# Samples' new keys in blocks of 32, both prompt blocks at once through the spatial product, values normalised further ahead

## The chip, the cores and the metric

The kernel runs on one core of a Trainium2 chip. The metric is the device time of one execution in microseconds (us), the median of several runs. A profile of one execution gives the time of each instruction on TensorE (PE, with its weight loads as PEld), VectorE (DVE), ScalarE (ACT), GpSimd (POOL) and the DMA queues.

## The reference, cut to what matters

One inference step of a two-layer encoder, for one prompt of 256 positions and 8 samples of 16 new positions each, with 128 cached positions behind every sample. All data are float32. Layer 0 has 8 forgetting-attention heads and 8 stick-breaking heads; layer 1 is a gMLP with a causal spatial product over chunks of 128 positions.

```python
# layer 0, samples: keys are the 128 cached ones and the sample's own 16 new ones
k_all = concatenate([cache_fox_k, gk], axis=1)
v_all = concatenate([cache_fox_v, gv], axis=1)
go = fox_core(gq, k_all, v_all, F_all[:, P:], F_all, qpos, kpos)   # softmax(q k^T + forget bias, causal) v
to = sb_core(tq, sk_all, sv_all, qpos, kpos)                       # stick-breaking weights, strictly causal
hs = hs + (concatenate([go * silu(gz), to * silu(tz)], -1) @ w_out0)

# layer 1
u, v, z = split(rmsnorm(h, norm1_g) @ w_in1)      # 4096 columns each
v = layernorm(v, ln_g, ln_b)                      # over the 4096 columns
mixed = einsum('gts,bnsgc->bntgc', tril(w_sp), v) + b_sp   # 16 groups of 256 columns
h = h + (u * mixed * silu(z)) @ w_out1
```

A sample sees only its own 16 new keys, so of the 128 x 128 scores between all samples' new queries and new keys only eight blocks of 16 x 16 on the diagonal count; the rest is masked.

## The kernel before, in words

**Tokens.** The 384 tokens stand as NT = 3 blocks of 128: two of the prompt, one with all samples (8 x 16). `P` is 128, `T` is 384.

**Dense products.** `dense_nat` multiplies all 384 tokens with 512 columns of a weight. To keep float32 accuracy every operand is split into a high part (fp32r) and the rest, and three products are summed (high x high, high x low, low x high). `wunit` loads a 128 x 512 piece of the weight (`raw`), ScalarE copies it to `whi` (L84), VectorE subtracts to `wlo` (L86), and `products` issues the matmuls at L100, L101 and L102: two pieces a step, three token blocks, 18 matmuls of 512 columns. `whi` and `wlo` have four buffers each.

**Order.** The instructions are traced in program order and then scheduled: each engine gets a fixed order from a simulation, in which an instruction that stands earlier in the program goes first among those that are ready. `tc.issue_after(x)` queues what its block traces on x's engine behind x. Work of the attention is hooked between the steps of later dense products (`between`, `at(g, what, kp, f)`).

**Layer 0.** `quad(g)` does four heads: it projects k, q, z and v and hooks `scores` and `attended` for pairs of heads, (0, 1) and (2, 3). `head` is a generator that is run in pieces:
- `scores`: the cached keys are turned (L625), the prompt scores go to the bank `sc` (L630, L631). In the bank `sd` the samples' new keys give one 128 x 128 product (L633), and the cached keys give four products in tiles of 32 output rows, one for each pair of samples (L636). `scores` runs L630 to L633 inside `issue_after(last_product[0])`. A bias with the mask (`md`, for the samples, 384 wide) is added, the softmax or the stick-breaking runs over 384 columns, and the weights (six blocks of 128, three for the prompt and three for the samples) go to memory (`wd`) and come back in 32-row pieces (`blk`, L496).
- `attended`: `blk` is turned to `PT` (L674). Samples' outputs go to the part `od` of a bank: first the new values by four products of 32 output rows over all 128 new keys (L681), then the cached values, eight more (L685). Then come the prompt's (L687 to L689), and the gate is multiplied in.

**Layer 1.** The eight groups of 512 columns of v are projected first and kept in `vt`, with their statistics. `normalise(c)` loads gain and bias of a group to a slot (L786, L787), does six steps on VectorE (L790, L791) and stores the samples' part. Then, for each group c:
1. the spatial weights of two of the 16 groups are loaded, masked, turned and split (`spatial_weights`),
2. z is projected and put through silu to `gate` (L862), u is projected and multiplied in (L865),
3. `normalise(c + 1)`,
4. the spatial product of the split values `vh`, `vl` for the three token blocks (L885, L886, L887; 256 columns each), whose result is multiplied into `gate` (L890),
5. `gate` is turned by VectorE and 16 small transfers on POOL (`turn`, L125 and L128), split into two slots (`ghi`, `glo`), and `split_values(c + 1)` fills `vh` and `vl`, which have one buffer each,
6. after groups 2, 4 and 6, `out1` multiplies two finished groups with the output weight (evicted at L830).

**Slots.** One pool of 16 slots (`slot()`, 6 KB a partition each) holds, in layer 1, the normalised input in 8 slots, the residual `h1` in 4, `ghi` and `glo` in one each per group until `out1` has read them, and the gain and bias of a group in one.

Of the kernel before, what the change touches and what calls it, by code (L numbers as in the profile page):

```python
# [15 lines left out]
P = 128  # L16
DM = 2048
KT = DM // P
NT = 3
# [18 lines left out]
def tile_hybrid_step(  # L38
# [117 lines left out]

    with ExitStack() as l0:
        lc = l0.enter_context(tc.tile_pool(name="l0c", bufs=1, reuse_waits="tile"))  # L160
        lp = l0.enter_context(tc.tile_pool(name="l0p", bufs=2, reuse_waits="tile"))
# [306 lines left out]
        def quad(g):  # L468
# [11 lines left out]
            def scores(pair):  # L480

                for hh in pair:
                    hs = slice(hh * P, hh * P + P)
                    own[hh] = head(g, h0 + hh, own["k"][:, hh], lambda hs=hs: own["v"][:, :, hs], own["q"][:, hh],
                                   keys_of[4 * g + hh], lambda n=4 * g + hh: values_of[n], lambda hs=hs: own["z"][:, :, hs])
                wd = own[pair] = dram.tile([2, 6, P, P], F32, name=nm("wd"))
                for hh in pair[::-1]:
                    next(own[hh])
                with tc.issue_after(last_product[0]):
                    for hh in pair:  # L490
                        next(own[hh])
                for j, hh in enumerate(pair):
                    own[hh].send(wd[j])
                blk = own["blk", pair] = slot(F32).rearrange("p (j x) -> p j x", j=2)
# [110 lines left out]
        def head(g, h, kT, values, qT, kc, vc, gate):  # L605
            fox = g < 2
            mp, md = masks[0 if fox else 1]
            if fox:

                fb = lp.tile([P, 2, T], F32, tag="fb", name=nm("fb"))  # L610
                fc = lp.tile([P, P], F32, tag="fc", bufs=1, name=nm("fc"))
                G.dma_start(fb[:, 0, :2 * P], nFd[h, :2 * P].partition_broadcast(P))
                G.dma_start(fb[:, 0, 2 * P:], nFd[h, :P].partition_broadcast(P))
                G.dma_start(fb[:, 1, 2 * P:], nFd[h, 2 * P:].partition_broadcast(P))
                G.dma_start(fc, nFcd[:, h, :].unsqueeze(1).broadcast_to([8, 16, P]))
                G.tensor_tensor(out=fb[:, 0, :], in0=fb[:, 0, :], in1=mp, op=ALU.add)
                G.tensor_tensor(out=fb[:, 1, 2 * P:], in0=fb[:, 1, 2 * P:], in1=md[:, 2 * P:], op=ALU.add)
                G.tensor_tensor(out=fb[:, 1, :2 * P].rearrange("p (s k) -> p s k", s=2), in0=md[:, :2 * P].rearrange("p (s k) -> p s k", s=2),
                                in1=fc.unsqueeze(1).broadcast_to([P, 2, P]), op=ALU.add)
                mp, md = fb[:, 0, :], fb[:, 1, :]  # L620

            KTt = []
            for hf in range(2):
# [6 lines left out]
            PE.matmul(sc[:, :2 * P].rearrange("p (t k) -> p t k", t=2), lhsT=qT[:, P:2 * P], rhs=kT[:, :2 * P].rearrange("p (t k) -> p t k", t=2), start=True, stop=True)  # L630
            PE.matmul(sc[:, 2 * P:T], lhsT=qT[:, :P], rhs=kT[:, :P], start=True, stop=True)  # L631
            sd = bank()
            PE.matmul(sd[:, 2 * P:T], lhsT=qT[:, 2 * P:], rhs=kT[:, 2 * P:], start=True, stop=True)  # L633
            wd = yield
            for j in range(4):
                PE.matmul(sd[32 * j:32 * j + 32, :2 * P], lhsT=qT[:, 2 * P + 32 * j:2 * P + 32 * j + 32], rhs=KTt[j // 2][:, (j % 2) * 256:(j % 2) * 256 + 256],  # L636
                          start=True, stop=True)

            weights = lp.tile([P, 2 * T], F32, tag="pr", name=nm("pr"))
            rs = {}  # L640
            for dec, s in ((0, sc), (1, sd)):
                m = md if dec else mp
                blocks = [(0, T, 2)] if dec else [(0, 2 * P, 1), (2 * P, T, 0)]
                z = tmp("z")
                if fox:
                    st = lp.tile([P, 4], F32, tag="st", bufs=8, name=nm("st"))
                    for i, (a, e, tb) in enumerate(blocks):
                        V.scalar_tensor_tensor(out=z[:, a:e], in0=s[:, a:e], scalar=Fnat[:, tb, h:h + 1], in1=m[:, a:e], op0=ALU.add, op1=ALU.add)
                        V.tensor_reduce(out=st[:, i:i + 1], in_=z[:, a:e], axis=AX.X, op=ALU.max, negate=True)
                    pr = weights[:, dec * T:dec * T + T]  # L650
                    for i, (a, e, tb) in enumerate(blocks):
                        S.activation(pr[:, a:e], z[:, a:e], AF.Exp, bias=st[:, i:i + 1], accum_out=st[:, 2 + i:3 + i])
                    n = len(blocks)
                    V.reciprocal(out=st[:, 2:2 + n], in_=st[:, 2:2 + n])
                    for i, (a, e, tb) in enumerate(blocks):
                        rs[tb] = st[:, 2 + i:3 + i]
                else:
                    V.tensor_tensor(out=z, in0=s[:, :T], in1=m, op=ALU.add)
                    l = tmp("l")
# [8 lines left out]
                    pr = weights[:, dec * T:dec * T + T]  # L668
# [4 lines left out]
            PT = lp.tile([P, 2 * T], F32, tag="PT", name=nm("PT"))  # L673
# [4 lines left out]
            od, ot = ob[:, 2 * P:3 * P], ob[:, :2 * P]  # L678
            for j in range(4):
                js = slice(32 * j, 32 * j + 32)  # L680
                PE.matmul(od[js, :], lhsT=PD[:, 2 * P + 32 * j:2 * P + 32 * j + 32], rhs=vn[:, 2, :], start=True, stop=False)  # L681
            for s in range(2):
                for j in range(4):
                    js = slice(32 * j, 32 * j + 32)
# [80 lines left out]
    with ExitStack() as l1:  # L765
# [91 lines left out]
        for c in range(8):  # L857
# [5 lines left out]
            o = dense_nat(w_in1, 0, c * 512, hh_, hl_)  # L863
            for tb in range(NT):
                V.scalar_tensor_tensor(out=gate[:, tb, :], in0=o[tb], scalar=rstd[:, tb:tb + 1], in1=gate[:, tb, :], op0=ALU.mult, op1=ALU.mult)  # L865
            if c < 7:
                normalise(c + 1)
            else:

                for j in range(2):  # L870
                    fg = slot(F32)[:, :1024]
# [4 lines left out]
                for j, ck in enumerate(order[:3]):  # L876
                    aside[ck] = x[:, j, :]
                    G.dma_start(x[:, j, :], wlast(*ck))
            for tb in range(NT):
                m = bank()  # L880
                for i in range(2):
                    cs = slice(i * 256, i * 256 + 256)
                    (wh, wl), (vh, vl) = wTs[i], vhl
                    o = m[:, cs]
                    PE.matmul(o, lhsT=wh[:, tb // 2, :], rhs=vh[:, tb, cs], start=True, stop=False)  # L885
                    PE.matmul(o, lhsT=wh[:, tb // 2, :], rhs=vl[:, tb, cs], start=False, stop=False)  # L886
                    PE.matmul(o, lhsT=wl[:, tb // 2, :], rhs=vh[:, tb, cs], start=False, stop=True)  # L887
                for i in range(2):
                    gh = gate[:, tb, i * 256:(i + 1) * 256]
                    V.scalar_tensor_tensor(out=gh, in0=m[:, i * 256:(i + 1) * 256], scalar=bcol[:, tb // 2, 2 * c + i:2 * c + i + 1], in1=gh, op0=ALU.add, op1=ALU.mult)  # L890
# [123 lines left out]
```

## Time and profile before

| | |
|---|---|
| median of 3 runs | 1794.22 us (1794.2 to 1795.07) |
| profiled execution | 1795.94 us, its span 1794.2 us |
| granted TensorE clock | 0.999 |
| busy: PE / DVE / ACT / POOL | 1782.1 / 946.6 / 729.0 / 369.9 us |
| matmuls | 8623 |
| moved by DMA | 307.64 MB |

In the rows of the trace's timeline the columns are: start in us from the start of the span, duration in us, engine, line of the kernel, operation, out<-in by the program's names, shape and count; brackets give the idle time before it and what ended it. For a matmul `128*32` is rows x columns of the weights in the array, and `128x512` is the moving operand. A matmul of two float32 operands stands as two passes, so `x16` there is eight matmuls. Matmuls overlap in the pipeline, so a matmul is shown longer than the step to the next one. Where rows are grouped (`x3`), start is that of the first.

### The profile page before, as it was taken

Reading aid. Unit: us, or ns where it says so; the run is one execution under the profiler, and the core shown is the slowest. Engines: PE = TensorE matmul, PEld = TensorE weight load, DVE = VectorE, ACT = ScalarE, POOL = GpSimd, SP = SyncE. Lnnn points to the kernel's source line nnn. Section 1 sums busy time; section 2 is a strip of 40 time slices with the busy share of each in tenths; the row PEclk is TensorE's granted clock in tenths of the full one; section 3 lists DMA queues with packets and bytes.
Section 4 is the critical chain, followed back from the end, with each engine's and each line's share of the span. In section 5 each row is a group of like instructions: output and inputs, shape, how many; then the busy total and the mean of one; then the engine's idle time right before and its main releaser. Section 6 shows DMA issues by size and latency. Waiting matters only on the chain.

```text
span 1794.2 us, 24567 instructions
## 1 busy us (share of the span) xinstructions
PE 1782.1 (99%) x8623; PEld 1480.1 (82%) x8623; DVE 946.6 (53%) x1578; ACT 729.0 (41%) x1301; POOL 369.9 (21%) x544
## 2 busy tenths in 40 slices
PE   9999999999999999999999999999999999999998
PEld 8988878888888888888888888888888888888887
DVE  6437465457448455534434556455555464455366
ACT  5435354346337344433333333433333333433344
POOL 1516544223311211200300121220120210220020
PEclk9999999999999999999999999999999999999999
DMA  6868988868867877644444454454454554455553
GB/s 198 248 172 212 273 225 225 236 176 227 234 189 196 236 198 195 190 129 130 137 130 124 144 158 128 145 147 148 145 147 116 151 156 129 146 146 150 156 146 119
DMA packets 185772, 307.64 MB, mean 171 GB/s; under 512 B 22904, under 2 KB 63152, under 8 KB 185648
## 3 DMA queue, kind: packets, MB, share of 16 engines
q1 hardware_dynamic: 127696, 225.37, 42.6%
q0 software_dynamic: 25072, 63.53, 14.0%
q10 hardware_dynamic: 32880, 17.18, 3.2%
q8 instruction: 67, 1.10, 0.3%
q14 instruction: 57, 0.47, 0.1%
HBM read 269.23 MB, written 30.47 MB: 167 GB/s over the span
## 4 chain that ended last, share of the span: by engine, by line
PE 95%; DMA 2%; issue 1%; DVE 1%; POOL 1%; ACT 0%; POOLq 0%; DVEq 0%; ACTq 0%
PE d L100 29%; PE d L102 29%; PE d L101 29%; DMA slot<-in_sgu_ln_b_dram 1%; PE a L101 1%; PE a L100 1%; PE a L102 1%; DMA d<-gz 0%; PE a L636 0%; DMA slot<-d 0%; PE a L630 0%; PE a L886 0%; PE d L426 0%; PE a L685 0%; PE d L944 0%
## 5 line engine op out<-in xcount | busy, mean ns | idle before, releaser
L86 DVE TENSOR_TENSOR wlo<-raw,whi 128x512 fp32r<-128x512 f32 x784 | 538.9, 696 | 722.2 <-ACT whi L84 721.9
L101 PE MATMUL d<-wlo,slot 128*128 128x512 f32 x2349 | 912.1, 390 | 1.7 <-DVE wlo L86 1.7
L102 PE MATMUL d<-whi,slot 128*128 128x512 f32 x2349 | 911.5, 389 | 0.0
L84 ACT ACTIVATE whi<-raw 128x512 fp32r<-128x512 f32 x784 | 493.1, 631 | 900.7 <-PE d L102 838.2
L100 PE MATMUL d<-whi,slot 128*128 128x512 f32 x2349 | 822.4, 390 | 0.0
L101 PEld LDWEIGHTS d<-wlo,slot 128*128 128x128 f32 x2349 | 441.0, 188 | 93.7 <-DVE wlo L86 3.2
L100 PEld LDWEIGHTS d<-whi,slot 128*128 128x128 f32 x2349 | 440.6, 188 | 93.9 <-issue 0.8
L102 PEld LDWEIGHTS d<-whi,slot 128*128 128x128 f32 x2349 | 440.9, 188 | 91.1
L128 POOL DMA_DIRECT2D gTt<-trn x128 | 77.9, 617 | 315.1 <-issue 190.1
L398 POOL DMA_DIRECT2D slot<-d x48 | 44.0, 923 | 140.8 <-DVE wlo L86 54.6
L837 POOL DMA_DIRECT2D wr<-in_w_sp_dram x64 | 34.9, 552 | 113.1 <-DVE wT L841 99.0
L496 POOL DMA_DIRECT2D slot<-wd x32 | 29.3, 922 | 103.5 <-DMA wd<-pr 41.1
L830 DVE TENSOR_TENSOR slot<-d,slot 128x512 f32<-128x512 f32 x48 | 32.4, 689 | 13.8 <-PE d L102 13.8
L786 POOL DMA_DIRECT2D slot<-in_sgu_ln_g_dram x8 | 4.6, 569 | 133.4 <-PE d L102 133.4
L457 POOL DMA_DIRECT2D kcache<-in_cache_sb_k_dram x32 | 24.9, 785 | 32.6 <-DVE KT L625 32.6
L457 POOL DMA_DIRECT2D kcache<-in_cache_fox_k_dram x32 | 25.0, 787 | 22.1 <-DVE KT L625 20.9
L712 POOL DMA_DIRECT2D blk<-h1d x12 | 10.9, 918 | 70.3 <-DMA h1d<-slot 59.9
L802 POOL DMA_DIRECT2D bcol<-in_b_sp_dram x1 | 1.2, 1176 | 116.1 <-DVE w L801 116.1
L780 POOL TENSOR_SCALAR rsv<-mvr 128x3 f32<-128x3 f32 x1 | 0.5, 538 | 108.1 <-DVE mvr L779 108.1
L777 DVE BATCH_NORM_STATS2 stats<-vt 128x6 f32<-128x512 f32 x24 | 16.2, 689 | 11.6 <-ACT vt L776 11.6
L865 DVE SCALAR_TENSOR_TENSOR gate<-d,rstd,gate 128x512 f32<-128x512 f32 x24 | 17.4, 749 | 7.3 <-PE d L102 7.3
L862 ACT ACTIVATE gate<-d,rstd 128x512 f32<-128x512 f32 x24 | 16.5, 689 | 11.2 <-PE d L102 11.1
(247 smaller groups left out, 1270.9 us busy)
## 6 DMA issues: line engine op xcount, KB each, us to landing
raw<-in_w_in_dram SPq DMA_DIRECT2D x640, 256.0 KB, 2.8
raw<-in_w_out_dram SPq DMA_DIRECT2D x189, 256.0 KB, 3.3
slot<-d POOLq DMA_DIRECT2D x48, 192.0 KB, 5.7
d<-slot ACTq DMA_DIRECT2D x24, 256.0 KB, 3.7
wd<-pr ACTq DMA_DIRECT2D x16, 384.0 KB, 5.7
slot<-wd POOLq DMA_DIRECT2D x32, 192.0 KB, 5.8
gTt<-trn POOLq DMA_DIRECT2D x128, 48.0 KB, 3.5
kcache<-in_cache_fox_k_dram POOLq DMA_DIRECT2D x32, 128.0 KB, 5.9
```

Source lines behind the costliest of these rows:

```text
L84: highs.append(S.activation(hi, raw, AF.Copy).ins)
L86: splits.append(V.tensor_tensor(out=lo, in0=raw, in1=f32(hi), op=ALU.subtract).ins)
L100: PE.matmul(o, lhsT=his[k][:, t], rhs=hi[:, 0, :], start=(k == first), stop=False)
L101: PE.matmul(o, lhsT=his[k][:, t], rhs=lo[:, 0, :], start=False, stop=False)
L102: mm = PE.matmul(o, lhsT=los[k][:, t], rhs=hi[:, 0, :], start=False, stop=(k == last))
L128: G.dma_start(dst[32 * j:32 * j + 32, :, 32 * a:32 * a + 32], trn[32 * a:32 * a + 32, :, 32 * j:32 * j + 32])
L398: r = G.dma_start(blk[32 * j:32 * j + 32].rearrange("p h (a d) -> p (h a) d", d=32), d[:, :, 32 * j:32 * j + 32].rearrange("h (a p) d -> p ...
L457: G.dma_start(k[32 * j:32 * j + 32].rearrange("p (b d) -> p b d", d=32), (c_fox_k, c_sb_k)[n // 8][:, :, n % 8, 32 * j:32 * j + 32].rearra ...
L496: G.dma_start(blk[32 * j:32 * j + 32].rearrange("p j (a d) -> p (j a) d", d=32), wd[:, :, :, 32 * j:32 * j + 32].rearrange("j x (a p) d -> ...
L830: evicted = V.tensor_tensor(out=h1[c][:, tb, :], in0=o[tb], in1=h1[c][:, tb, :], op=ALU.add)
L837: G.dma_start(wr[js, 0, :].rearrange("p (a s) -> p a s", s=32), w_sp[g, :, js].rearrange("(a p) s -> p a s", p=32))
L865: V.scalar_tensor_tensor(out=gate[:, tb, :], in0=o[tb], scalar=rstd[:, tb:tb + 1], in1=gate[:, tb, :], op0=ALU.mult, op1=ALU.mult)
```

## The change

Layer 0. The mask `md` for the samples is 288 wide: 256 columns for the cached keys and 32 for the new ones (`TW = 2 * P + 32`). A row's 32 new keys are those of its own block of 32 rows (two samples); the eight 32 x 32 blocks of the two masks are copied there by POOL from a full 128 x 128 mask. The new keys' scores are four products of 32 rows by 32 columns, which now stand behind the generator's second `yield`, directly before the products with the cached keys. The weights of the new keys are turned in place by VectorE (a transposition of 32 x 32 blocks) to `own`, and only five blocks of 128 go through memory. The new values are then taken by four products over 32 keys each, on the diagonal.

Layer 1. For each half of a group one spatial product takes both prompt blocks (2 x 256 columns) at once; the sample block keeps its own. `normalise` runs for group 1 in group 0, for 2 and 3 in group 1, for 4 and 5 in group 3, for 6 and 7 in group 5.

```diff
+    TW = 2 * P + 32
...
-            md = lc.tile([P, T], F32, name=f"md{strict}")
+            md = lc.tile([P, TW], F32, name=f"md{strict}")
...
-            mdn = md[:, 2 * P:].rearrange("p (b q) -> p b q", q=16)
+            new = lp.tile([P, 2 * T], F32, tag="PT", name=nm("new"))[:, :P]
+            V.memset(new, 0.0)
+            mdn = new.rearrange("p (b q) -> p b q", q=16)
...
+            for j in range(4):
+                js = slice(32 * j, 32 * j + 32)
+                G.tensor_copy(md[js, 2 * P:], new[js, js])
...
-                wd = own[pair] = dram.tile([2, 6, P, P], F32, name=nm("wd"))
+                wd = own[pair] = dram.tile([2, 5, P, P], F32, name=nm("wd"))
...
-                G.dma_start(fb[:, 1, 2 * P:], nFd[h, 2 * P:].partition_broadcast(P))
+                G.dma_start(fb[:, 1, 2 * P:TW], nFd[h, 2 * P:].rearrange("(j k) -> j k", k=32).unsqueeze(1).broadcast_to([4, 32, 32]))
...
             sd = bank()
-            PE.matmul(sd[:, 2 * P:T], lhsT=qT[:, 2 * P:], rhs=kT[:, 2 * P:], start=True, stop=True)
             wd = yield
+            for j in range(4):
+                js = slice(2 * P + 32 * j, 2 * P + 32 * j + 32)
+                PE.matmul(sd[32 * j:32 * j + 32, 2 * P:TW], lhsT=qT[:, js], rhs=kT[:, js], start=True, stop=True)
             for j in range(4):
                 PE.matmul(sd[32 * j:32 * j + 32, :2 * P], ...
...
-                blocks = [(0, T, 2)] if dec else [(0, 2 * P, 1), (2 * P, T, 0)]
+                blocks = [(0, TW, 2)] if dec else [(0, 2 * P, 1), (2 * P, T, 0)]
...
-            nc.scalar.dma_start(wd.rearrange("x q k -> q x k"), weights.rearrange("q (x k) -> q x k", k=P))
+            nc.scalar.dma_start(wd.rearrange("x q k -> q x k"), weights[:, :5 * P].rearrange("q (x k) -> q x k", k=P))
+
+            own = lp.tile([P, 32], F32, tag="own", bufs=4, name=nm("own"))
+            V.transpose(out=own, in_=weights[:, 5 * P:])
             blk = yield
...
             for j in range(4):
                 js = slice(32 * j, 32 * j + 32)
-                PE.matmul(od[js, :], lhsT=PD[:, 2 * P + 32 * j:2 * P + 32 * j + 32], rhs=vn[:, 2, :], start=True, stop=False)
+                PE.matmul(od[js, :], lhsT=own[js, :], rhs=vn[js, 2, :], start=True, stop=False)
...
-            if c < 7:
-                normalise(c + 1)
-            else:
+            for n in {0: (1,), 1: (2, 3), 3: (4, 5), 5: (6, 7)}.get(c, ()):
+                normalise(n)
+            if c == 7:
...
-            for tb in range(NT):
+            for i in range(2):
+                cs = slice(i * 256, i * 256 + 256)
+                (wh, wl), (vh, vl) = wTs[i], vhl
+                bcols = bcol[:, :, 2 * c + i:2 * c + i + 1]
                 m = bank()
...
+                o = m.rearrange("p (t c) -> p t c", t=2)
+                PE.matmul(o, lhsT=wh[:, 0, :], rhs=vh[:, :2, cs], start=True, stop=False)
+                PE.matmul(o, lhsT=wh[:, 0, :], rhs=vl[:, :2, cs], start=False, stop=False)
+                PE.matmul(o, lhsT=wl[:, 0, :], rhs=vh[:, :2, cs], start=False, stop=True)
+                V.scalar_tensor_tensor(out=gate[:, :2, cs], in0=o, scalar=bcols[:, 0, :], in1=gate[:, :2, cs], op0=ALU.add, op1=ALU.mult)
+            m = bank()
+            for i in range(2):
...
+                PE.matmul(m[:, cs], lhsT=wh[:, 1, :], rhs=vh[:, 2, cs], start=True, stop=False)
+                PE.matmul(m[:, cs], lhsT=wh[:, 1, :], rhs=vl[:, 2, cs], start=False, stop=False)
+                PE.matmul(m[:, cs], lhsT=wl[:, 1, :], rhs=vh[:, 2, cs], start=False, stop=True)
...
```

More of the change, by code (lines that the diff above doesn't have):

```diff
@@ L493, in scores @@
                     own[hh].send(wd[j])
-                blk = own["blk", pair] = slot(F32).rearrange("p (j x) -> p j x", j=2)
+                blk = own["blk", pair] = slot(F32)[:, :2 * 5 * P].rearrange("p (j x) -> p j x", j=2)
                 for j in range(4):
@@ L613, in head @@
                 G.dma_start(fb[:, 0, 2 * P:], nFd[h, :P].partition_broadcast(P))
-                G.dma_start(fb[:, 1, 2 * P:], nFd[h, 2 * P:].partition_broadcast(P))
+                G.dma_start(fb[:, 1, 2 * P:TW], nFd[h, 2 * P:].rearrange("(j k) -> j k", k=32).unsqueeze(1).broadcast_to([4, 32, 32]))
                 G.dma_start(fc, nFcd[:, h, :].unsqueeze(1).broadcast_to([8, 16, P]))
                 G.tensor_tensor(out=fb[:, 0, :], in0=fb[:, 0, :], in1=mp, op=ALU.add)
-                G.tensor_tensor(out=fb[:, 1, 2 * P:], in0=fb[:, 1, 2 * P:], in1=md[:, 2 * P:], op=ALU.add)
+                G.tensor_tensor(out=fb[:, 1, 2 * P:TW], in0=fb[:, 1, 2 * P:TW], in1=md[:, 2 * P:], op=ALU.add)
                 G.tensor_tensor(out=fb[:, 1, :2 * P].rearrange("p (s k) -> p s k", s=2), in0=md[:, :2 * P].rearrange("p (s k) -> p s k", s=2),
                                 in1=fc.unsqueeze(1).broadcast_to([P, 2, P]), op=ALU.add)
-                mp, md = fb[:, 0, :], fb[:, 1, :]
+                mp, md = fb[:, 0, :], fb[:, 1, :TW]
             KTt = []
@@ L637, in head @@
                           start=True, stop=True)
-            weights = lp.tile([P, 2 * T], F32, tag="pr", name=nm("pr"))
+            weights = lp.tile([P, T + TW], F32, tag="pr", name=nm("pr"))
             rs = {}
@@ L642, in head @@
                 m = md if dec else mp
-                blocks = [(0, T, 2)] if dec else [(0, 2 * P, 1), (2 * P, T, 0)]
-                z = tmp("z")
+                blocks = [(0, TW, 2)] if dec else [(0, 2 * P, 1), (2 * P, T, 0)]
+                n = TW if dec else T
+                z = tmp("z")[:, :n]
+                pr = weights[:, dec * T:dec * T + n]
                 if fox:
@@ L649, in head @@
                         V.tensor_reduce(out=st[:, i:i + 1], in_=z[:, a:e], axis=AX.X, op=ALU.max, negate=True)
-                    pr = weights[:, dec * T:dec * T + T]
                     for i, (a, e, tb) in enumerate(blocks):
                         S.activation(pr[:, a:e], z[:, a:e], AF.Exp, bias=st[:, i:i + 1], accum_out=st[:, 2 + i:3 + i])
-                    n = len(blocks)
-                    V.reciprocal(out=st[:, 2:2 + n], in_=st[:, 2:2 + n])
+                    V.reciprocal(out=st[:, 2:2 + len(blocks)], in_=st[:, 2:2 + len(blocks)])
                     for i, (a, e, tb) in enumerate(blocks):
@@ L657, in head @@
                 else:
-                    V.tensor_tensor(out=z, in0=s[:, :T], in1=m, op=ALU.add)
-                    l = tmp("l")
+                    V.tensor_tensor(out=z, in0=s[:, :n], in1=m, op=ALU.add)
+                    l = tmp("l")[:, :n]
                     S.activation(l, z, AF.Abs)
@@ L667, in head @@
                     V.tensor_tensor(out=z, in0=z, in1=l, op=ALU.add)
-                    pr = weights[:, dec * T:dec * T + T]
                     S.activation(pr, z, AF.Exp)
-            nc.scalar.dma_start(wd.rearrange("x q k -> q x k"), weights.rearrange("q (x k) -> q x k", k=P))
+            nc.scalar.dma_start(wd.rearrange("x q k -> q x k"), weights[:, :5 * P].rearrange("q (x k) -> q x k", k=P))
+            own = lp.tile([P, 32], F32, tag="own", bufs=4, name=nm("own"))
+            V.transpose(out=own, in_=weights[:, 5 * P:])
             blk = yield
-            PT = lp.tile([P, 2 * T], F32, tag="PT", name=nm("PT"))
+            PT = lp.tile([P, 2 * T], F32, tag="PT", name=nm("PT"))[:, :5 * P]
             yield V.transpose(out=PT, in_=blk)
@@ L878, in tile_hybrid_step @@
                     G.dma_start(x[:, j, :], wlast(*ck))
-            for tb in range(NT):
+            for i in range(2):
+                cs = slice(i * 256, i * 256 + 256)
+                (wh, wl), (vh, vl) = wTs[i], vhl
+                bcols = bcol[:, :, 2 * c + i:2 * c + i + 1]
                 m = bank()
[L881 to L890, printed above, removed]
+                o = m.rearrange("p (t c) -> p t c", t=2)
[5 more added lines that the diff above has]
+            for i in range(2):
+                cs = slice(i * 256, i * 256 + 256)
+                (wh, wl), (vh, vl) = wTs[i], vhl
+                PE.matmul(m[:, cs], lhsT=wh[:, 1, :], rhs=vh[:, 2, cs], start=True, stop=False)
+                PE.matmul(m[:, cs], lhsT=wh[:, 1, :], rhs=vl[:, 2, cs], start=False, stop=False)
+                PE.matmul(m[:, cs], lhsT=wl[:, 1, :], rhs=vh[:, 2, cs], start=False, stop=True)
+            for i in range(2):
+                cs = slice(i * 256, i * 256 + 256)
+                V.scalar_tensor_tensor(out=gate[:, 2, cs], in0=m[:, cs], scalar=bcol[:, 1, 2 * c + i:2 * c + i + 1], in1=gate[:, 2, cs], op0=ALU.add, op1=ALU.mult)
             gT = lp.tile([P, NT * 4, P], F32, tag="gTt", bufs=1, name=nm("gTt"))
```

## The prediction, made before the changed kernel was run

> **What bounds the kernel now.** I read the page first (share of each engine, the chain that ended last), then who waited for whom on TensorE, then TensorE's timeline around the places that the change touches.
>
> ```profile
> span 1794.2 us, 24567 instructions
> PE 1782.1 (99%) x8623; PEld 1480.1 (82%) x8623; DVE 946.6 (53%) x1578; ACT 729.0 (41%) x1301; POOL 369.9 (21%) x544
> PE 95%; DMA 2%; issue 1%; DVE 1%; POOL 1%; ACT 0%; POOLq 0%; DVEq 0%; ACTq 0%
> ```
>
> TensorE is busy 99% of the span and is 95% of the chain. A change moves the time only through the time TensorE spends on its own instructions or through the few places where it waits. Those places, from the waits of TensorE:
>
> ```profile
> PE d L101 <- DVE wlo L86: 1.7, 3, 1.3
> PE a L886 <- DVE vl L91: 0.5, 3, 0.2
> ```
>
> VectorE is late six times: three times with the low half of a weight (L101; one of them, the 1.3, is in layer 0), three times with the low half of the values (L886, spatial product). These waits are not the whole loss, since a matmul's shown duration is longer than its step. So the steps from start to start are the measure.
>
> ```profile
> 1073.49 0.84 PE L100 MATMUL d<-whi,slot 128*128 128x512 f32 x3
> ...
> 1077.57 0.84 PE L100 MATMUL d<-whi,slot 128*128 128x512 f32 x3
> ...
> 1082.24 0.28 PE L886 MATMUL a<-vl,wTh 128*128 128x256 f32 x1
> ...
> 1082.60 0.28 PE L886 MATMUL a<-vl,wTh 128*128 128x256 f32 x1
> ...
> 1082.96 0.40 PE L100 MATMUL d<-whi,slot 128*128 128x512 f32 x1
> ```
>
> Between the first two rows lie the 18 matmuls of one pair of weight units: 4.08 / 18 = 0.227 us for 512 columns. Between the next two lie three spatial matmuls: 0.36 / 3 = 0.12 us for 256 columns, a little more than half of 0.227. The last row is a dense product in the middle of the spatial ones: the scheduler lets TensorE take whatever is ready.
>
> **Layer 1, the spatial product.** A group has 18 matmuls of 256 columns: 18 x 0.12 = 2.16 us. After, the two prompt blocks go through together as 2 x 3 matmuls of 512 columns, and the sample block keeps 2 x 3 of 256: 6 x 0.227 + 6 x 0.12 = 2.08 us. Over 8 groups that is -0.6 us. On VectorE four evictions replace six; VectorE is not the bound there, so I cost that at nothing.
>
> **Layer 1, normalising earlier.** What stalls TensorE now, once in every two groups:
>
> ```profile
> 1451.14 0.28 PE L885 MATMUL a<-vh,wTh 128*128 128x256 f32 x1
> 1451.61 0.50 PE L101 MATMUL d<-wlo,slot 128*128 128x512 f32 x1 [0.20 <-DVE wlo L86]
> 1451.95 0.40 PE L102 MATMUL d<-whi,slot 128*128 128x512 f32 x1
> ...
> 1452.43 0.28 PE L885 MATMUL a<-vh,wTh 128*128 128x256 f32 x1
> 1452.88 0.39 PE L886 MATMUL a<-vl,wTh 128*128 128x256 f32 x1 [0.17 <-DVE vl L91]
> 1453.10 0.28 PE L887 MATMUL a<-vh,wTl 128*128 128x256 f32 x1
> ```
>
> ```profile
> 1446.03 2.08 DVE L790 SCALAR_TENSOR_TENSOR vt<-vt,mvr,slot 128x512 f32<-128x512 f32 x3 [0.84 <-DMA slot<-in_sgu_ln_g_dram]
> 1448.94 0.75 DVE L791 SCALAR_TENSOR_TENSOR vt<-vt,rsv,slot 128x512 f32<-128x512 f32 x1 [0.83 <-DMA slot<-in_sgu_ln_b_dram]
> 1449.61 0.69 DVE L86 TENSOR_TENSOR wlo<-raw,whi 128x512 fp32r<-128x512 f32 x1
> ...
> 1452.14 0.69 DVE L91 TENSOR_TENSOR vl<-vt,vh 128x512 fp32r<-128x512 f32 x1
> ```
>
> ```profile
> 1442.20 0.58 POOL L786 DMA_DIRECT2D slot<-in_sgu_ln_g_dram  x1 [39.69 <-PE d L102]
> ```
>
> Read backwards: the spatial product waits for `vl`, that for the six normalising steps at 1446 to 1452, those for the gain and bias loads, and those stood 39.69 us in POOL's queue for a free slot. A count of slots explains it: 8 for the layer's input, 4 for h1, 2 for each finished group not yet through `out1`. Of the 16, group 2 already needs 12 + 4, so the seventeenth, the gain of group 3, waits until `out1` has read. Groups 4 and 6 repeat it. After, groups 2 and 3 are normalised in group 1 (14 slots in use, two more fit), and 4, 5 and 6, 7 in groups 3 and 5, where `out1` has just given four back. Each moved step takes along six VectorE instructions of about 0.75 us, two loads and one store on POOL. They stand in the program behind the dense product of their own group, so its weight splits go first. The 0.69 of L86 twice per 4.08 us leaves VectorE room, and the values are due two dense products later.
>
> What it is worth: 1451.14 to 1451.61 is 0.47 where 0.12 is due, and 1451.61 to 1451.95 is 0.34 where 0.227 is: 0.46 lost. 1452.43 to 1453.10 is 0.67 where 0.24 is due: 0.43 lost. The waits say three of the second kind and, without the long one in layer 0, two of the first: 3 x 0.43 + 2 x 0.46 = 2.2 us. Bounds: 0 (as much burst elsewhere, twelve steps at a time) to -2.2. I take -2.2: what is late next are the copies of the gate, which feed `out1` a dense product later.
>
> **Layer 0, scores of the samples' new keys.**
>
> ```profile
> 140.50 0.39 PE L633 MATMUL a<-kT,qT 128*128 128x128 f32 x2
> 140.72 0.60 PE L630 MATMUL a<-kT,qT 128*128 128x256 f32 x2
> ...
> 141.38 0.39 PE L633 MATMUL a<-kT,qT 128*128 128x128 f32 x2
> 141.69 1.07 PE L636 MATMUL a<-KT,qT 128*32 128x256 f32 x16
> 142.69 0.50 PE L100 MATMUL d<-whi,slot 128*128 128x512 f32 x1
> 143.03 0.39 PE L101 MATMUL d<-wlo,slot 128*128 128x512 f32 x1
> ```
>
> ```profile
> 71.27 0.54 PE L364 MATMUL a<-ones,clf 128*8 128x1 f32 x16
> 71.67 0.71 PE L374 MATMUL a<-sums,clf 128*8 128x128 f32 x5
> ```
>
> L633 is the product that goes: 140.50 to 140.72, 0.22 us a head in two passes, 16 x 0.22 = -3.5 us. In its place come four matmuls of 32 columns (eight passes) in the same 32-column tiles as L636. L636 does 16 passes of 256 columns in 1.00 us, four tiles at once, so 0.25 for four passes; an eighth of the columns is an estimate of 0.03. The other end is L364: 16 passes of one column in 0.40 us, one after the other, 0.10 for four. A head has two such fours: 16 x 2 x (0.03 to 0.10) = +1.0 to +3.2 us. I take 0.04, near L636, whose tiles they share: +1.3. Sum of this part: -2.2, between -2.5 and -0.3.
>
> **What a change of tile costs.** From 141.38 to 141.69 is 0.31 where 0.22 is due: entering the narrow tiles costs 0.09, and about 0.02 more in their first passes. Leaving, 142.69 to 143.03 is 0.34 where 0.227 is due, and the attention shows both halves:
>
> ```profile
> 460.54 0.43 PE L681 MATMUL a<-vnat,PT 128*32 128x128 f32 x8
> 460.78 0.62 PE L685 MATMUL a<-vcache,PT 128*32 128x128 f32 x16
> 461.22 0.40 PE L681 MATMUL a<-vnat,PT 128*32 128x128 f32 x8
> 461.44 0.62 PE L685 MATMUL a<-vcache,PT 128*32 128x128 f32 x16
> 461.99 0.49 PE L687 MATMUL a<-vnat,PT 128*128 128x128 f32 x2
> 462.31 0.39 PE L688 MATMUL a<-vnat,PT 128*128 128x128 f32 x2
> 462.53 0.39 PE L689 MATMUL a<-vnat,PT 128*128 128x128 f32 x2
> ```
>
> L685 without a change takes 0.44 (460.78 to 461.22), before leaving 0.55: 0.11. The first wide pair takes 0.32 where 0.22 is due: 0.10. So an excursion into narrow tiles and back costs 0.11 + 0.20 = 0.31 us, a change between two kinds of narrow tile about 0.11. [...]
>
> **Layer 0, values of the new keys.** L681 becomes four products of 32 rows by 32 columns on the diagonal: still eight passes of 128 columns, 0.22 us a head if the four run side by side as now. But the tile now differs from L685's, and the operand `own` is turned on the chip right after the scores instead of coming back through memory some 30 us later. So this product is ready early, and the scheduler may issue it alone. Joined to L685 in the order of the program, a pair of heads has three more changes (in, across, back across): 8 x 3 x 0.11 = +2.6. Issued as one excursion per pair: 8 x 0.31 = +2.5. One per four heads: 4 x 0.31 = +1.2. One per product: 64 x 0.31 = +20. The scores of the new keys lose a hold, too: L633 stood behind the last dense product by an explicit edge, and L636 behind L633 through their bank; now neither does. For the second pair of each group of heads, whose keys and queries are long turned, I add one excursion: 4 x 0.31 = +1.2 (0 to 5).
>
> **Beside the path.** The weights go to memory and back in five blocks instead of six, and the sample's softmax runs over 288 columns instead of 384: less for DMA, VectorE, ScalarE and POOL, none of which TensorE waits for here, so nothing. One small transpose a head is added. POOL gets eight small copies for the masks:
>
> ```profile
> L340 POOL DMA_DIRECT2D wf<-in_w_in_dram x1 | 1.3, 1336 | 24.6 <-DVE wf L337 24.6
> L289 POOL TENSOR_SCALAR_AFFINE_SELECT md<-md 128x128 f32<-128x128 f32 x6 | 1.8, 333 | 0.0
> ```
>
> Eight at no more than 0.33 are 2.7 us, ahead of 24.6 us of idle time. Nothing.
>
> **Sum.** -0.6 - 2.2 - 2.2 + 2.5 + 1.2 = -1.3 us. The profiled execution took 1795.94 us (span 1794.2 and 1.7 around it), 0.1% over the median of 1794.22. Against the median: 1792.9 us.
>
> **Rivals.**
> 1. Few excursions: the products of four heads go together and the scores stay with L636: -0.6 - 2.2 - 2.2 + 1.2 = -3.8, and perhaps without the stall of 1.3 in layer 0, whose place the shorter transfers may move: 1789 to 1790.4. For it: all four heads' operands are ready when the values are evicted. Against: gaps in TensorE's schedule hold few instructions.
> 2. Many excursions (slower). The mechanism is row 1082.96: ready products fill gaps one by one, dense ones between them. In wide tiles this is free; here each return costs 0.31. Savings are 5.0 us, so it decides from 16 excursions on, and from 28 on the kernel is over 0.2% slower. At 40 (a third of the 128 new small products): -5.0 + 12.4 = +7.4, 1801.6. Against: in the attention all 48 passes of a pair went in one piece before.
> 3. The diagonal products do not run side by side, though they share one bank in disjoint partitions: 8 x 0.11 instead of 0.22, +0.66 a head, 16 x 0.66 = +10.6, 1803.5. No row of before has row tiles. [...]
> 4. The early normalising does not do what it says: the twelve steps push the weight splits late elsewhere, and the 2.2 us stay: 1795.1.
>
> **How the numbers follow.** A difference under 0.2% (3.6 us) can hardly be told from none here. The forecast's case (6 to 16 excursions) has 0.46, rival 1 0.24, rival 2 0.12, rival 3 0.05, rival 4 0.13. Faster: rival 1, 0.24. Same: forecast and rival 4, 0.59. Slower: 0.17. The range 1787.5 to 1799 takes in rivals 1 and 4 with the bounds of the scores, and the lower part of rival 2; what is left out is rival 3, the upper part of rival 2, and a little below. The forecast's own range is 1790.6 to 1795.
>
> **What would show it.** In the profile after: no L786 standing 40 us in POOL's queue, and no step of TensorE over 0.13 us within the spatial products; 512-column spatial matmuls 0.227 apart; four passes of 32 columns in some 0.04 us; the diagonal products eight passes in 0.22; the number of times TensorE changes between tiles in layer 0, each 0.11 in and 0.20 out. The prediction is wrong if that number is far from 12 on top of before's, if row tiles go one at a time, or if a new wait of TensorE of more than 1 us stands anywhere.

## The result, and the profile after

The changed kernel takes 1804.34 us (median of 6 runs, 1802.24 to 1805.35), against 1794.45 us for the kernel before (6 runs, 1794.2 to 1795.07): ratio 1.0051, 95% interval 1.0042 to 1.0061, slower by 9.9 us. Forecast was 1792.9 us, faster by 0.1%. (Here and below a ratio is taken over all runs and has a 95% interval; it need not equal the quotient of the two medians.) The profiled execution after took 1805.35 us, its span is 1803.6 us, 9.4 us over the one before.

The page after, its span, engines and chain, and then the waits of TensorE (total us, times, longest):

```profile
span 1803.6 us, 24696 instructions
PE 1788.9 (99%) x8671; PEld 1478.5 (82%) x8671; DVE 940.2 (52%) x1580; ACT 724.8 (40%) x1301; POOL 369.0 (20%) x552
PE 97%; issue 1%; DVE 1%; DMA 1%; ACT 0%; POOL 0%; POOLq 0%; DVEq 0%; ACTq 0%
...
PE d L101 <- DVE wlo L86: 5.2, 2, 2.7
PE a L201 <- DVE ones L134: 1.1, 1, 1.1
```

The shares say nothing: TensorE is 99% busy, as before. The first wait, for the low half of a weight, says where to look. Before it was 1.7 us in three pieces; now it is 5.2 us in two. The small waits for `vl` (0.5 us in three) are gone.

Where the 9.4 us lie is read from the 7191 dense matmuls of 512 columns that both kernels have: the start of the k-th one, counted from the first matmul of the execution, in the one trace minus the other. The difference moves only at a few places:

| part of the execution | us, after minus before |
|---|---|
| start, up to the first dense product | +2.2 |
| scores of the samples, 8 pairs of heads x -0.32 | -2.6 |
| attended values, 8 pairs of heads | +5.7 |
| a stall of before in layer 0, absent after | -1.6 |
| layer 1 | +5.7 |
| sum | +9.4 |

**Layer 1.** One of its two stalls, at the start of group 3, in TensorE's timeline:

```profile
1263.02 0.84 PE L100 MATMUL d<-whi,slot 128*128 128x512 f32 x3
1266.57 0.67 PE L101 MATMUL d<-wlo,slot 128*128 128x512 f32 x1 [2.71 <-DVE wlo L86]
1267.04 0.63 PE L102 MATMUL d<-whi,slot 128*128 128x512 f32 x1
1267.46 0.63 PE L100 MATMUL d<-whi,slot 128*128 128x512 f32 x1
...
1270.02 0.45 PE L100 MATMUL d<-whi,slot 128*128 128x512 f32 x1
1270.32 0.39 PE L101 MATMUL d<-wlo,slot 128*128 128x512 f32 x1
```

The three matmuls of the first row start 0.227 apart, so the next was due at 1263.70 and starts at 1266.57: 2.87 us lost. Then nine matmuls take 3.75 us (1266.57 to 1270.32) where 9 x 0.227 = 2.04 are due: 1.71 more. Most of them are 0.427 apart instead of 0.227. Busy time by engine in the stretch shows the same, its column after POOL's being the mean granted clock, 0.83:

```profile
1262.90:1273.00 10.10, 7.39 (x26) 5.66 (x25) 8.54 (x14) 2.17 (x4) 1.09 (x2) 0.83 0.51 161
```

From 1266.75 to 1270.14 alone the granted clock is 0.50. One such stall costs 4.6 us. The second one, at 1468 in group 5, costs 4.4 by the same count. The timelines of VectorE, POOL and ScalarE show what is behind it:

```profile
1256.09 0.68 DVE L86 TENSOR_TENSOR wlo<-raw,whi 128x512 fp32r<-128x512 f32 x1
1259.86 2.08 DVE L803 SCALAR_TENSOR_TENSOR vt<-vt,mvr,slot 128x512 f32<-128x512 f32 x3 [3.09 <-DMA slot<-in_sgu_ln_g_dram]
1261.85 2.07 DVE L804 SCALAR_TENSOR_TENSOR vt<-vt,rsv,slot 128x512 f32<-128x512 f32 x3
1263.84 2.07 DVE L803 SCALAR_TENSOR_TENSOR vt<-vt,mvr,slot 128x512 f32<-128x512 f32 x3
1265.83 1.29 DVE L86 TENSOR_TENSOR wlo<-raw,whi 128x512 fp32r<-128x512 f32 x2
```

```profile
1255.09 0.56 POOL L799 DMA_DIRECT2D slot<-in_sgu_ln_g_dram  x1 [15.94 <-PE d L102]
...
1459.82 0.56 POOL L799 DMA_DIRECT2D slot<-in_sgu_ln_g_dram  x1 [28.07 <-PE d L102]
```

```profile
1260.27 1.31 ACT L84 ACTIVATE whi<-raw 128x512 fp32r<-128x512 f32 x2 [4.58 <-PE d L102]
```

Read backwards: the split (L86) at 1265.83 releases TensorE. It stands in VectorE's fixed order behind nine normalising steps, six us of work. These stand behind the gain load, which VectorE waits 3.09 us for. That load is issued at 1255.09, because its slot is freed by the last matmul of `out1`, and in VectorE's order the steps stand right behind `out1`'s work and one more split. From 1256.77 to 1265.83 no weight is split: 9.06 us, where four buffers of `wlo`, all full, would last at most 2 x 4.08 us. Here TensorE runs dry 6.93 us after the last split, at 1263.70. ScalarE's row shows that no split was due at first: it copies no weight until 1260.27, when a buffer comes free. So the wait for the gain costs nothing while it lasts; it pushes the nine steps into the time in which splits are due. Group 5 repeats it: all the waiting for the gain is

```profile
who waited for it (us, times):
  DVE vt L803: 5.9, 2
```

Group 1 is another place with twelve steps. Its loads were issued at 1068.34, before the steps came up, so nothing waits; at most six steps stand in a row, and TensorE does not wait there.

**Layer 0.** The scores of a pair of heads, and then the values of the second pair in group 2:

```profile
143.09 0.39 PE L640 MATMUL a<-kT,qT 128*128 128x128 f32 x2
143.41 0.27 PE L645 MATMUL a<-kT,qT 128*32 128x32 f32 x8
143.49 0.62 PE L647 MATMUL a<-KT,qT 128*32 128x256 f32 x8
143.93 0.24 PE L645 MATMUL a<-kT,qT 128*32 128x32 f32 x8
143.99 0.62 PE L647 MATMUL a<-KT,qT 128*32 128x256 f32 x8
144.53 0.50 PE L100 MATMUL d<-whi,slot 128*128 128x512 f32 x1
```

```profile
458.62 0.40 PE L694 MATMUL a<-vnat,own 32*32 32x128 f32 x2
...
463.25 0.41 PE L694 MATMUL a<-vnat,own 32*32 32x128 f32 x6
463.59 0.65 PE L698 MATMUL a<-vcache,PT 128*32 128x128 f32 x16
464.17 0.42 PE L694 MATMUL a<-vnat,own 32*32 32x128 f32 x8
464.52 0.65 PE L698 MATMUL a<-vcache,PT 128*32 128x128 f32 x16
465.09 0.49 PE L700 MATMUL a<-vnat,PT 128*128 128x128 f32 x2
```

The eight passes of 32 columns take 0.06 to 0.08 us a head. In the values, each change between the tiles 32*32 and 128*32 costs 0.11 to 0.14: L694 to L698 is 0.35 (464.17 to 464.52) for eight passes that took 0.22 to 0.24 before, L698 to L694 0.58 (463.59 to 464.17) for sixteen that took 0.44. One product (458.62, two passes) has been issued alone, 4.6 us ahead of its three fellows, between dense products; the next dense product starts 0.42 late and the one behind it 0.11 more, 0.53 in all. By the starts of the dense matmuls a joined pair of heads costs 0.37 over before's and such a lone piece 0.55. In the first group of heads all own products of the second pair went alone, in four pieces, two of them here:

```profile
191.63 0.40 PE L694 MATMUL a<-vnat,own 32*32 32x128 f32 x2
191.96 0.50 PE L100 MATMUL d<-whi,slot 128*128 128x512 f32 x1
...
201.46 0.42 PE L694 MATMUL a<-vnat,own 32*32 32x128 f32 x8
201.81 0.50 PE L100 MATMUL d<-whi,slot 128*128 128x512 f32 x1
```

One product of two passes holds the next dense one for 0.33 us, four products of eight passes for 0.35: the four run side by side.

### The profile page after: what moved, and what is told of

Its sections match the earlier page's. It is cut to its first block, busy times and chain, and to the rows that moved or that the text cites. A ratio compares the mean times of both kernels' runs of the same rounds, so it can differ in the third digit from the quotient of the medians.

```text
span 1803.6 us, 24696 instructions
## 1 busy us (share of the span) xinstructions
PE 1788.9 (99%) x8671; PEld 1478.5 (82%) x8671; DVE 940.2 (52%) x1580; ACT 724.8 (40%) x1301; POOL 369.0 (20%) x552
## 4 chain that ended last, share of the span: by engine, by line
PE 97%; issue 1%; DVE 1%; DMA 1%; ACT 0%; POOL 0%; POOLq 0%; DVEq 0%; ACTq 0%
PE d L100 29%; PE d L101 29%; PE d L102 29%; PE a L102 1%; PE a L100 1%; PE a L101 1%; DMA slot<-in_sgu_ln_g_dram 1%; PE a L698 1%; PE a L694 0%; PE a L647 0%; PE a L639 0%; DVE vt L803 0%; PE d L435 0%; PE d L967 0%; PE d L966 0%
## 5 line engine op out<-in xcount | busy, mean ns | idle before, releaser
L86 DVE TENSOR_TENSOR wlo<-raw,whi 128x512 fp32r<-128x512 f32 x784 | 535.8, 692 | 728.6 <-ACT whi L84 723.4
L790 DVE BATCH_NORM_STATS2 stats<-vt 128x6 f32<-128x512 f32 x24 | 16.4, 690 | 13.3 <-ACT vt L789 13.3
L789 ACT ACTIVATE vt<-d,rstd 128x512 f32<-128x512 f32 x24 | 16.4, 690 | 13.3 <-PE d L102 13.3
```

Of the source, the lines that this page charges most:

```text
L86: splits.append(V.tensor_tensor(out=lo, in0=raw, in1=f32(hi), op=ALU.subtract).ins)
```

## The experiments

Theory A: two causes that add. In layer 1 VectorE's fixed order holds the weight splits behind normalising steps that themselves wait for late gain loads; in layer 0 the own values' tile costs a change each time, joined or alone. The rivals, B to F, stand in the expectations. Where two kernels are compared across two sets of runs, it is by their ratios to the kernel before.

**The two halves apart.** `l0_only` is the layer 0 part of the diff on the kernel before, `l1_only` the layer 1 part, `spatial_only` the spatial product of both prompt blocks without the earlier normalising:

```diff
# spatial_only: of the layer 1 part only this
-            for tb in range(NT):
+            for i in range(2):
...
+                PE.matmul(o, lhsT=wh[:, 0, :], rhs=vh[:, :2, cs], start=True, stop=False)
...
# l1_only: this as well
-            if c < 7:
-                normalise(c + 1)
+            for n in {0: (1,), 1: (2, 3), 3: (4, 5), 5: (6, 7)}.get(c, ()):
+                normalise(n)
```

> Layer 0's part of the change alone (layer 1 as before). Theory A (the loss has separate places that add up): against before -2.6 us in the scores, +5.7 in the attention's changes of tile, -1.6 from the vanished stall at 236 us, so about +1.6: 1796 us; 1798 if the later full clock at the start (+2.1 in the profile of after) comes with the masks. Rival B (the new stalls of layer 1 are only there because layer 0 shifted the schedule): all of the loss appears here or none can be told apart, 1800 us or more, or below 1794.

> Layer 1's part of the change alone (layer 0 as before). Theory A: two stalls of TensorE of about 3 us after out1 of groups 0 to 1 and 2 to 3, each followed by some eight matmuls at 0.427 us, and without the small stalls of before: about +5.7, 1800 us. Rival B: no such stalls without layer 0's part, -3.0, 1791.5 us.

> Only the spatial product with both prompt blocks at once; normalising one group ahead as before. Theory A: 8 x 0.08 = -0.6 us and the small stalls of before stay: 1793.8 us. Rival C (the wider spatial product or its wider eviction delays VectorE and makes the new stalls): 1798 us or more.

Measured, against the kernel before at 1794.57 us (25 runs): `l0_only` 1797.31, ratio 1.0014 [1.0005, 1.0024]; `l1_only` 1801.28, 1.0038 [1.0023, 1.0053]; `spatial_only` 1794.99, 1.0007 [0.9997, 1.0017]. The two halves sum to +2.7 + 6.7 = +9.4, against +9.9 together: they add, and rival B falls. The traces say it by place: the values' +5.7 and the scores' -2.6 stand whole in `l0_only`, layer 1's +5.7 in `l1_only`. The waits of TensorE in `l1_only`, and in `spatial_only`:

```profile
PE d L101 <- DVE wlo L86: 6.3, 3, 2.8
```

```profile
PE d L101 <- DVE wlo L86: 0.3, 1, 0.3
```

Two of the three in `l1_only` are the layer 1 stalls, 5.1 us; the third is the stall of before in layer 0. So the long wait belongs to the normalising, not to the spatial product alone, and rival C falls. (The earlier normalising without the new spatial product was not run.) The spatial product alone moves nothing that can be told: by the starts of the dense matmuls layer 1 is 0.9 us shorter than before, but in `l0_only`, whose layer 1 is before's, it is 1.4 us shorter too. Before's small stalls, on which I had rested a gain of 2.2, are themselves not in every execution. Nor is the stall of 1.6 us in layer 0: it is absent in `spatial_only`, whose layer 0 is untouched and whose matmuls there stand in the same order.

**The wait or the burst.** `hooked` is the changed kernel with the loads hooked to a step of z and the steps spread, two at a time, over later steps of u. `burst` keeps the loads of `hooked` and releases all twelve steps at one step of u.

```diff
-            o = dense_nat(w_in1, 0, 2 * CW + c * 512, hh_, hl_)
+            gs, todo = steps(*{0: (1,), 1: (2, 3), 3: (4, 5), 5: (6, 7)}.get(c, ()))
+            o = dense_nat(w_in1, 0, 2 * CW + c * 512, hh_, hl_, between={4: lambda: [next(g) for g in gs] and None} if gs else None)
...
-            o = dense_nat(w_in1, 0, c * 512, hh_, hl_)
+            o = dense_nat(w_in1, 0, c * 512, hh_, hl_, between={2 + 2 * i: f for i, f in enumerate(todo)})     # hooked
+            o = dense_nat(w_in1, 0, c * 512, hh_, hl_, between={6: lambda: [f() for f in todo] and None} if todo else None)     # burst
```

> The changed kernel, but the same groups are normalised in six steps spread over the steps of the u product (two VectorE instructions behind the weight splits of each step), their loads hooked into the z product. Theory A (VectorE's fixed order puts a wait for the gain and nine normalising instructions ahead of the next weight split): the stalls of 3 us and the slow matmuls behind them go, and layer 1 gains 3 against before instead of losing 5.7: 1804.3 - 8.7 = 1795.6 us. Rival D (twelve normalising instructions in one group are too much for VectorE wherever they stand): stays at 1800 us or more.

> As the kernel with six spread steps, but all twelve normalising instructions are released at one step of the u product; their loads are hooked into the z product, so they have landed. Theory A1 (the wait for the gain, 3.1 us with the weight splits queued behind it, makes the stall): 1796 us, as with spread steps. Rival D1 (nine normalising instructions in a row, 6.2 us, are enough): three stalls of TensorE of 1.5 us or more, 1800 to 1803 us.

Measured: `hooked` 1796.09 us, ratio 1.0003 [0.9993, 1.0012]; `burst` 1794.73, ratio 0.9999 [0.999, 1.0008] (before in its runs 1795.08). Both take back the layer 1 loss: by the starts of the dense matmuls layer 1 is 3.3 us shorter than before in both, against 5.7 longer in the changed kernel. The difference, 9.0, is what the two stalls cost (4.6 + 4.4). In neither does TensorE wait for `wlo` at all. The gain load of `burst` on POOL, and VectorE's steps:

```profile
1252.94 0.56 POOL L799 DMA_DIRECT2D slot<-in_sgu_ln_g_dram  x1 [15.94 <-PE d L102]
```

```profile
1290.91 4.06 DVE L804 SCALAR_TENSOR_TENSOR vt<-vt,mvr,slot 128x512 f32<-128x512 f32 x6
1294.88 1.41 DVE L805 SCALAR_TENSOR_TENSOR vt<-vt,rsv,slot 128x512 f32<-128x512 f32 x2
1296.21 0.69 DVE L86 TENSOR_TENSOR wlo<-raw,whi 128x512 fp32r<-128x512 f32 x1
```

The load is issued as late as in the changed kernel, right behind `out1`. Only the steps are elsewhere, 38 us behind it, and wait for nothing. Eight in a row hold the splits for 5.30 us (1290.91 to 1296.21), and TensorE does not notice. So a burst of eight is affordable there: rival D falls, and D1 as far as eight steps in another place can say. That the 3.09 us of waiting is what runs the buffers dry is worked out, not isolated: nine steps from 1256.77 on, without the wait, would have ended at 1262.74, before TensorE ran dry at 1263.70 (an estimate from the rows above). `burst` takes away the wait and also moves the steps to another place; the same place without the wait, and the wait without the burst, were not tried.

**The own values in a wide tile.** `wide` is the changed kernel with the own weights turned into a 128 x 128 tile that is zero beside its four diagonal blocks, so that a head has one 128-wide product, both heads' first:

```diff
-            own = lp.tile([P, 32], F32, tag="own", bufs=4, name=nm("own"))
-            V.transpose(out=own, in_=weights[:, 5 * P:])
+            own = owns[h % 4]
+            for j in range(4):
+                js = slice(32 * j, 32 * j + 32)
+                V.transpose(out=own[js, js], in_=weights[js, 5 * P:])
...
-            for j in range(4):
-                js = slice(32 * j, 32 * j + 32)
-                PE.matmul(od[js, :], lhsT=own[js, :], rhs=vn[js, 2, :], start=True, stop=False)
+            PE.matmul(od, lhsT=own, rhs=vn[:, 2, :], start=True, stop=False)
+            yield
```

> The changed kernel, but the weights of the new keys are turned into the diagonal blocks of a 128 x 128 tile that is zero elsewhere, and one wide product per head (128 rows by 128 columns, 0.22 us) takes the new values, both heads' ahead of the cached ones. Theory A (what layer 0 lost are changes of tile: across, back, and lone products): the attention costs what it cost before, -5.7 against the changed kernel: 1798.6 us. Rival E (the loss comes from the product being ready early, wherever and in whatever tile it is issued): 1802 us or more.

Measured: 1798.97 us, ratio 1.0027 [1.0016, 1.0038]. The values no longer cost anything: by the starts of the dense matmuls they are +0.1 us over before, not +5.7, and rival E falls. Layer 1's wait stays, as it should:

```profile
PE d L101 <- DVE wlo L86: 5.8, 2, 2.9
```

**What the 5.7 us of the values are made of.** Two variants of `hooked`: `own_last` puts the own products behind the cached ones of the same head, `grouped` puts the own products of both heads ahead of the cached ones of both.

```diff
# own_last
-            for j in range(4):
-                js = slice(32 * j, 32 * j + 32)
-                PE.matmul(od[js, :], lhsT=own[js, :], rhs=vn[js, 2, :], start=True, stop=False)
             for s in range(2):
...
+            for j in range(4):
+                js = slice(32 * j, 32 * j + 32)
+                PE.matmul(od[js, :], lhsT=own[js, :], rhs=vn[js, 2, :], start=False, stop=True)
# grouped
-                    for hh in pair:
-                        next(own[hh])
+                    for _ in range(2):
+                        for hh in pair:
+                            next(own[hh])
...
+            yield
             for s in range(2):
```

> The kernel with the spread normalising, and in the attention the products of the samples' own new values behind those with the cached values (same bank, same eight passes) instead of ahead of them. The computation is the same. Theory A (part of the attention's loss is pieces issued alone, before the cached weights are back: one in each of three groups of heads, four in the first): they have nothing to wait for now but their place, so no row of 32*32 stands apart from 128*32 rows, and of the 5.7 us that the attention lost only the joined part stays, 8 pairs x 0.37 = 3.0 us: against the kernel before the attention loses 3.0 us in the profile, and the median is about 2.7 us under that of the spread normalising, ratio to before 0.9990 (1793.3 against 1796.1). Theory F (the loss is the change of tile in itself, wherever the pieces stand): nothing moves, attention +5.7, ratio 1.0003.

> The kernel with the spread normalising, and in the attention the own products of both heads of a pair ahead of the cached products of both. The computation is the same. Theory A (a joined change between the two narrow tiles costs about 0.11 us, three of them a pair): one instead of three a pair, 8 x 2 x 0.11 = 1.8 us less than the spread normalising, ratio to before 0.9993 (1794.3); a joined pair has 0.15 us over before's instead of 0.37. The pieces issued alone stay, or there are more of them (two heads' own products are now first): each excursion of its own that is added costs 0.3 to 0.55. Theory F (the loss is not the changes but the diagonal products themselves): a joined pair keeps its 0.37, ratio 1.0003.

Measured, before at 1794.6 us: `own_last` 1792.55, ratio 0.9987 [0.9978, 0.9996]; `grouped` 1794.83, ratio 0.9997 [0.9989, 1.0006]. By the starts of the dense matmuls the values cost +3.8 in `own_last` and +4.5 in `grouped`, against +5.7. Both expectations were met in part. `grouped` saves 0.24 per joined pair in the last three groups of heads, as two changes of 0.12 should; the first group kept its old order and lost 0.2 more. (The trace of `grouped` also has a wait of 0.7 us for `whi` at 687, with a loss of 1.1 that stands in no other trace and is not in the 4.5.) `own_last` has no lone pieces of the own products left, which saves 1.5 us in the first group; in each of the three others a lone piece of the cached values came instead, here in the last:

```profile
586.52 0.43 PE L695 MATMUL a<-vcache,PT 128*32 128x128 f32 x8
588.47 0.43 PE L695 MATMUL a<-vcache,PT 128*32 128x128 f32 x8
588.82 0.42 PE L698 MATMUL a<-vnat,own 32*32 32x128 f32 x8
589.17 0.65 PE L695 MATMUL a<-vcache,PT 128*32 128x128 f32 x16
589.75 0.42 PE L698 MATMUL a<-vnat,own 32*32 32x128 f32 x8
```

And one joined pair of `grouped`, with one change between narrow tiles where the changed kernel has three:

```profile
605.55 0.63 PE L695 MATMUL a<-vnat,own 32*32 32x128 f32 x14
606.11 1.08 PE L700 MATMUL a<-vcache,PT 128*32 128x128 f32 x32
607.12 0.49 PE L702 MATMUL a<-vnat,PT 128*128 128x128 f32 x2
```

So of the 5.7 of the changed kernel, by the starts, the six joined pairs of the last three groups are 6 x 0.37 = 2.22, their three lone pieces 3 x 0.55 = 1.65, and the first group, where four pieces went alone, 1.86.

**Both repairs, and the version that wins.** `b_hooked` is the kernel before with the new spatial product and the spread normalising; `wide_hooked` is the changed kernel with the wide own product and the spread normalising.

> Layer 0 as before; layer 1 with the wider spatial product and the normalising in six spread steps. Theory A: -0.6 for the product and -2.4 for the small stalls of before: 1791.2 to 1791.6 us. Rival: the spread instructions cost as much as the small stalls they replace, 1794 us.

> The changed kernel with both repairs: wide product of the new values, and six spread normalising steps. Theory A: -2.6 for the scores in blocks of 32 and -3.0 for layer 1 against before: 1788.9 us, faster than both kernels. Rival E: the attention's loss stays and eats both, 1794 us or more.

Measured, before at 1795.08 us (26 runs): `b_hooked` 1792.66, ratio 0.9988 [0.9979, 0.9997]; `wide_hooked` 1790.27, ratio 0.9972 [0.9961, 0.9982]. `wide_hooked` beats both kernels, the one before by 0.28%. The page of `wide_hooked` and all the waits of TensorE that it has left:

```profile
span 1789.0 us, 24559 instructions
...
PE a L201 <- DVE ones L134: 1.1, 1, 1.1
```

By the starts of the dense matmuls its layer 1 is 3.3 us shorter than before, its scores 2.6 shorter, its values 0.1 longer.

## Why the prediction was wrong, step by step

1. **The normalising: the step that failed.** It put -2.2 us (bounds 0 to -2.2); layer 1 as a whole came out at +5.7 where -2.8 stood, and two stalls of 4.6 and 4.4 us are what it had at nothing. Two of its sentences are wrong. "4, 5 and 6, 7 in groups 3 and 5, where `out1` has just given four back" counts slots rightly, but "just given back" means that the loads can be issued only when `out1` ends: 1255.09 and 1459.82, 4.8 and 4.5 us before the steps can start. And "its weight splits go first" took the place in the program for the place on the engine: in VectorE's order the steps stand behind `out1`'s last eviction and one split, ahead of most of the group's own splits. They run at 1259.86; the dense product that they stand behind in the program is evicted at 1323.12. The row of before that should have warned was among those quoted: L790 waiting 0.84 us for the same load. With one group's steps behind it the four buffers absorbed that; with two groups' and a wait of 3.09 they did not. The range took no loss into account at all: its upper end for this term was 0.
2. **Rival 4** named the place ("twelve steps push the weight splits late"), and had 0.13. It was priced as the gain forgone, 1795.1, not as a stall with its own cost. A row of steps alone was not enough to stall: `burst` has eight in a row, in another place, and layer 1 gains 3.3.
3. **The gain itself was there.** With the steps in another place layer 1 is 3.3 us shorter than before, where -0.6 - 2.2 was forecast. How much of it is the spatial product cannot be told: unchanged layer 1 code differed by 1.4 us between two executions.
4. **Values of the new keys: a term mis-sized.** +2.5 was forecast, for joined pairs or for one excursion a pair; measured 5.7, since both came. Six joined pairs cost 0.37 each, 2.22, near the forecast (a change across costs about 0.12, not 0.11). On top of them seven pieces went alone, three in the last groups (1.65) and four in the first, which cost 1.86 in all: its joined pair costs next to nothing more than before, whose two heads stood apart there. A lone piece costs 0.55, not 0.31, since its own two passes, hidden beside three fellows when joined, come on top when alone: 0.22 by an estimate, from the 0.22 that two passes of L701 take in the wide tile (465.42 to 465.64 after).
5. **Scores: right.** -2.2 forecast, 8 x -0.32 = -2.6 measured. Four passes of 32 columns take 0.03 to 0.04 us. The +1.2 for four excursions of these products came to nothing: none went alone.
6. **Rival 3 fell.** The diagonal products ran side by side here: eight passes alone hold the next product for 0.35 us (201.46), two for 0.33 (191.63). So the four row tiles, which write disjoint partitions of one bank, take together 0.02 us more than one alone. No run shows the 8 x 0.11 of this rival, one product after the other.
7. **Rival 2** (many excursions) had the mechanism of the lone pieces but not their number: seven separate pieces in all, not 40. Seven lies in the forecast's own range of 6 to 16; it was their price that was off.
8. **What would show it.** Its last test, "a new wait of TensorE of more than 1 us", is the one that came: 2.71 and 2.48 us. Its first failed in part: the gain load, now L799, still stands 15.94 and 28.07 us in POOL's queue for a slot.

The start, +2.2 us, belongs to no step of the prediction, and whether the change has a part in it stays open. `wide` and `wide_hooked` have the same start in their code, and theirs are at -0.1 and +2.2 against before. But of the eight traces with the layer 0 part six are 1.4 to 2.2 us late, and of the four without it, the one before among them, none is more than 0.4.

## What to carry to other kernels

A load that was issued when a buffer came free reached the work that needed it 4.5 to 4.8 us later here; such work must stand at least that far behind on an engine with a fixed order, or everything queued behind it is late too. When work is moved earlier on an engine that feeds the bound, look where the fixed order puts it, not where the program does, and set the sum of its wait and its burst against the buffers that cover it. Narrow tiles paid for every change of tile here (0.11 to 0.14 us between the two narrow ones): a wider product with zeros that stays in the tile of the dense products can be cheaper than four narrow ones with a quarter of the cells (the values in `wide` +0.1 us over before, in the changed kernel +5.7).

## What the runs showed of the hardware that was not expected

Each of the two stalls of TensorE in layer 1 cost more than half as much again afterwards: 1.71 us behind 2.87 lost, 1.72 behind 2.64. The matmuls behind both start up to 0.427 us apart instead of 0.227, and the granted clock is 0.50 for 3.39 us (1266.75 to 1270.14, and 1471.53 to 1474.92). The idle times ahead of that were 2.71 and 2.48 us; what lowers the clock, and after how long a wait, no run shows. The start varies, too. In the trace before, three matmuls of the first dense product take 0.93 us at 6.12; in the one after they take 1.62 at 6.31, and those at 9.64 are still slow:

```profile
6.12 0.93 PE L253 MATMUL d<-whi,slot 128*128 128x512 f32 x3 [0.36 <-DVE slot L228]
```

```profile
6.31 1.62 PE L256 MATMUL d<-whi,slot 128*128 128x512 f32 x3
...
9.64 1.32 PE L256 MATMUL d<-wlo,slot 128*128 128x512 f32 x3
10.80 0.40 PE L100 MATMUL d<-whi,slot 128*128 128x512 f32 x1
```

That is the +2.2 us of the table. The granted clock is 1.00 from 6 to 12 us in both traces, so the later full clock that the expectation of `l0_only` names for it is not shown; the slow matmuls are. Between `wide` and `wide_hooked`, with one code for the start, it differs by 2.3 us, as much as the smaller effects here: two profiles should have their starts taken out before they are compared to the microsecond.
